# A decoder trunk on one core: the Newton steps of the final norm go from GpSimd to VectorE, and their mean squares get four buffers

## The chip, the cores and the metric

The kernel runs on one core of one Trainium2 chip. The metric is the device time of one execution in microseconds, the median of several runs; lower is better. Engines are called TensorE (PE in the profile), VectorE (DVE), ScalarE (ACT), GpSimd (POOL) and SyncE (SP). PEld is TensorE's weight load.

## The reference

One decoder layer over 2048 tokens of 1024 features: a token mixer with three head groups, then a hierarchical mixture of 32 SwiGLU experts, two for each token, then a final RMSNorm. Only the last two matter here:

```python
def rms_norm(x, g):
    xf = x.astype(jnp.float32)
    y = xf * lax.rsqrt(jnp.mean(xf * xf, axis=-1, keepdims=True) + RMS_EPS)
    return (y * g.astype(jnp.float32)).astype(x.dtype)
...
    hid = jax.nn.silu(xb @ w_gate[e]) * (xb @ w_up[e])
    return hid @ w_down[e]
...
    x = x + gt2 * hier_moe(h, router_grp_w[l], router_grp_b[l], router_exp_w[l],
                           router_exp_b[l], exp_w_gate[l], exp_w_up[l], exp_w_down[l])
return rms_norm(x, final_norm_g)
```

## The kernel before

The stages before the experts (projections, the three mixers, output projection, routing) end at about 1950 us of 3079 and are not touched. The rest is the expert stage.

**Experts.** The 32 experts are ordered by how many tokens they have, and large and small ones alternate; each has a fixed capacity, from 240 down to 66 x 2 rows for the large ones and 88 to 128 for most of the small ones. Tokens sit on the partitions, so an expert with over 128 rows has its tokens in two pieces (18 experts), one with up to 128 in one piece (14 experts). For each expert its rows of the normalised input are gathered (`gather`, line 1866), transposed on TensorE (`transpose`), multiplied by the gate and up weights (`gate_up` with line 1957 and 1959 for large experts, `gate_up_few` with line 1931 for small ones), and by the down weights (`down`, lines 162 to 164).

**Weights.** Every expert loads 12 pieces of 512 KB on SyncE's queue into a ring of 11 staging buffers, `wraw` (lines 1903 and 1918). For large experts, and for every expert's down weights, ScalarE writes a rounded high part `wh` (line 1907) and VectorE the remainder `wl` (line 1908), into rings of 8; after the remainder the staging buffer is free for the next load. Small experts use their raw gate and up pieces, eight of the eleven buffers, straight from the staging ring.

**Draining.** The gate and up products of a large expert leave PSUM by a ScalarE copy and a VectorE add into `ga_` (lines 1963 and 1964); the PSUM tiles `pg` are rings of two, which both kinds of expert share.

**The running sum and the final norm.** `yp_d` is a table in DRAM with the residual of every token. For an expert, `partial` gathers the rows of it (line 1992, on GpSimd's queue), `down` puts the expert's weighted product in `y`, and `add` (lines 1997 to 2011) adds the two (VectorE, line 2001), scatters the sum back (GpSimd, line 2004), squares it on ScalarE with the row sum in `sx` (line 2009), and turns `sx` into a mean plus epsilon (line 2010). The inverse square root comes from `rsqrt_`: a seed by integer arithmetic on VectorE (lines 61 and 62) and three Newton rounds of four instructions (lines 64 to 67) on 128 x 2 numbers. `finish`, called one expert later, multiplies by the root and the gain (VectorE, line 2017) and scatters to the output (GpSimd, line 2018), for the tokens for which this was the second expert.

**Order.** Each engine runs its instructions in a fixed order, which a list scheduler chooses when the kernel is built; semaphores hold each instruction until what it needs is there. Tiles are buffers in rings: the scheduler places the first write of a tile where it expects its buffer to come free, so a memset that needs nothing else, such as that of `sx` (line 2007), lands right behind the last reader of the ring's buffer. Transfers into one DRAM table are ordered too: a scatter into `yp_d` waits until the one before it has landed.

Of the kernel before, what the change touches and what calls it, by code (L numbers as in the profile page):

```python
# [9 lines left out]
F32 = mybir.dt.float32  # L10
# [10 lines left out]
P = 128  # L21
# [19 lines left out]
def body(tc, x, c, ada_w, ada_b, norm1_g, w_in, gla_gate_w, gla_gate_b, gla_norm_g, dsa_norm_g,  # L41
# [6 lines left out]
    V, S, G, TE = nc.vector, nc.scalar, nc.gpsimd, nc.tensor  # L48
# [5 lines left out]
    def rsqrt_(pool, ms, n, tag, rows=P, eng=None):  # L54

        E = eng or V
        sh = pool.tile([P, n], I32, name="rs_i", tag=tag + "_i")
        y_ = pool.tile([P, n], F32, name="rs_y", tag=tag + "_y")
        t_ = pool.tile([P, n], F32, name="rs_t", tag=tag + "_t")
        sh, y, t, ms = sh[:rows], y_[:rows], t_[:rows], ms[:rows]  # L60
        V.tensor_scalar(sh, ms.bitcast(I32), 1, None, op0=OP.logical_shift_right)
        V.tensor_scalar(y.bitcast(I32), sh, -1, 0x5F3759DF, op0=OP.mult, op1=OP.add)
        for _ in range(3):
            E.tensor_mul(t, y, y)
            E.tensor_mul(t, t, ms)
            E.tensor_scalar(t, t, -0.5, 1.5, op0=OP.mult, op1=OP.add)
            E.tensor_mul(y, y, t)
        return y_
# [1752 lines left out]
    mx_ = es.enter_context(tc.tile_pool(name="mx", bufs=2))  # L1821
# [175 lines left out]
    def add(st, ys, parts, after=None):  # L1997

        n, nb, pl, ix, xgs = st
        for j, (y, part) in enumerate(zip(ys, parts)):  # L2000
            a = V.tensor_add(y[:n], y[:n], part[:n])  # L2001
            if after is not None:
                tc.add_manual_dep(a.ins, after.ins.name, ORDER, reason="products first")
            G.indirect_dma_start(out=yp_d[:, :], out_offset=bass.IndirectOffsetOnAxis(ap=ix[:n, 1, j:j + 1], axis=0),  # L2004
                                 in_=y[:n], in_offset=None, bounds_check=T - 1, oob_is_err=False)
        sx = mx_.tile([P, 2], F32, name="sx")
        V.memset(sx, 1.0)
        for j, (y, part) in enumerate(zip(ys, parts)):
            S.activation(part[:n], y[:n], AF.Square, accum_out=sx[:n, j:j + 1])
        V.tensor_scalar(sx, sx, 1.0 / D, EPS, op0=OP.mult, op1=OP.add)  # L2010
        return rsqrt_(mx_, sx, 2, "rsf", eng=G)

    def finish(st, ys, parts, rs):

# [44 lines left out]
    for r in range(NE + 1):  # L2059
# [33 lines left out]
        if r:  # L2093
            fin = sts[r - 1], ys, parts, add(sts[r - 1], ys, parts, after)
# [4 lines left out]
    with tc.For_i(0, na, 1) as it:  # L2099
        itm = mo3.tile([1, 4], I32, name="itm")  # L2100
        nc.sync.dma_start(itm, it_d[bass.ds(it, 1), :])
        _, (fv,) = nc.values_load_multi_w_load_instructions(itm[0:1, 0:1], min_val=0, max_val=1)
        with tc.If(fv > 0):
            kyi = mo3.tile([P, 1], I32, name="kyi")
            nc.sync.dma_start(kyi, it_d[bass.ds(it, 1), 3:4].to_broadcast([P, 1]))
            ky = mo3.tile([P, 1], F32, name="ky")
            V.tensor_copy(ky, kyi)
            row0 = nc.sync.value_load(itm[0:1, 1:2], min_val=0, max_val=NE * T - P)
            e = nc.sync.value_load(itm[0:1, 2:3], min_val=0, max_val=NE - 1)
            pl = mo3.tile([P, 1, 2, TW], F32, name="plo")  # L2110
            G.memset(pl, 0.0)
            load_list(pl[:, 0], row0, P)
            ix = lists(mo3, pl, 1, ky[:, :, None].to_broadcast([P, 1, 2]))
            st = gather(P, pl[:, 0], ix[:, :, 0])
            xT, todo = transpose(P, st, 1)
            for f_ in todo:
                f_()
            hid, rest = gate_up_few(P, xT, weights_raw(e))
            rest()
            parts = partial(st)  # L2120
            ys = down(st, hid, weights(e, 4))
            finish(st, ys, parts, add(st, ys, parts))
# [30 lines left out]
```

## Time and profile before

| | before |
|---|---|
| median of 3 runs | 3073.16 us (3071.29 to 3079.28) |
| the profiled execution: its own time | 3080.75 us |
| its span, first to last instruction | 3079.0 us |
| busy over the span: TensorE, VectorE, ScalarE, GpSimd | 2415.8, 2043.2, 1344.5, 1095.6 us |
| mean granted TensorE clock | 0.868 of full |
| bytes moved by DMA | 479.42 MB |

The profile is one execution. Its page gives the busy time of each engine, the waits (which engine stood still, for how long, and which instruction's end let it go on: "<- POOL rs_t L65" means that the wait ended with GpSimd's instruction of line 65), and the largest groups of instructions by source line. A line can be a helper's: lines 61 to 67 are `rsqrt_` wherever it is called from. Times in a timeline count from the start of the span.

### The profile page before, as it was taken

The numbers are of one execution on the slowest core, as the hardware profiler recorded it, in microseconds if no ns is written. First come the engines' busy times: TensorE is split into PE (matmuls) and PEld (weight loads), VectorE is DVE, ScalarE is ACT, GpSimd is POOL, SyncE is SP. The second block draws the span as 40 slices with busy tenths as digits, with TensorE's granted clock in tenths as the row PEclk, the third lists the DMA queues.
The fourth block names the chain that finished last, engine by engine and source line by source line (L and its number), as shares of the span: only waits on it lengthen the run. The fifth ranks groups of instructions, "written<-read, shape, count | busy, mean of one in ns | idle before, by whom it ended". The sixth has DMA issues, their size and how long they took to land. (4 is left out here: it accounts for less than half of the span.)

```text
span 3079.0 us, 38623 instructions
## 1 busy us (share of the span) xinstructions
PE 2415.8 (78%) x12571; PEld 1885.7 (61%) x12571; DVE 2043.2 (66%) x4392; ACT 1344.5 (44%) x2339; POOL 1095.6 (36%) x1139
## 2 busy tenths in 40 slices
PE   4989868778387999578988995887887878777783
PEld 3767546777266777366766784565565656554562
DVE  6578867989889645377875666565655656554673
ACT  2577867572122243466652221443433434333451
POOL 2211224346553422465443452133232333333333
PEclk9999868889587799689998996988898989888896
DMA  7222354343411432443215434877787877776861
GB/s 208 92 82 78 114 202 141 111 142 106 139 52 59 138 120 94 125 126 111 79 59 186 156 125 129 268 231 236 238 270 226 239 225 234 214 213 195 239 191 35
DMA packets 372280, 479.42 MB, mean 156 GB/s; under 512 B 84828, under 2 KB 271356, under 8 KB 371814
## 3 DMA queue, kind: packets, MB, share of 16 engines
q1 hardware_dynamic: 334501, 421.83, 43.3%
q0 software_dynamic: 37568, 55.05, 6.7%
q8 instruction: 100, 1.64, 0.2%
q14 instruction: 111, 0.90, 0.1%
HBM read 385.75 MB, written 112.23 MB: 162 GB/s over the span
## 5 line engine op out<-in xcount | busy, mean ns | idle before, releaser
L1908 DVE TENSOR_TENSOR wl<-wraw,wh 128x1024 fp32r<-128x1024 f32 x272 | 329.4, 1221 | 209.6 <-ACT wh L1907 202.7
L1907 ACT ACTIVATE wh<-wraw 128x1024 fp32r<-128x1024 f32 x272 | 286.2, 1054 | 335.6 <-PE pd L164 119.3
L1957 PE MATMUL pg<-xT,wh 128*128 128x416 f32 (+10 forms) x1152 | 342.6, 375 | 50.0 <-DVE ga__25564 L1964 13.9
L1931 PE MATMUL pg<-wraw,xT 128*120 128x512 f32 (+9 forms) x448 | 229.1, 675 | 131.1 <-DVE ga__25236 L1964 16.2
L1959 PE MATMUL pg<-xT,wl 128*128 128x208 f32 (+10 forms) x1152 | 290.1, 252 | 0.0
L1957 PEld LDWEIGHTS pg<-xT,wh 128*128 128x128 f32 x1152 | 232.9, 202 | 58.8 <-DVE ga__25564 L1964 14.3
L441 POOL TENSOR_TENSOR xx<-xr,xx 128x1024 fp32r<-128x1024 f32 x64 | 162.1, 2534 | 269.5 <-ACT xx L440 239.8
L1931 PEld LDWEIGHTS pg<-wraw,xT 128*120 128x120 f32 (+9 forms) x448 | 88.6, 202 | 263.0 <-issue 117.9
L1959 PEld LDWEIGHTS pg<-xT,wl 128*128 128x128 f32 x1152 | 236.4, 205 | 0.6
L2004 POOL DMA_INDIRECT yp_d<-y,ix x50 | 81.8, 1637 | 398.9 <-DVE y L2001 278.1
L255 DVE SCALAR_TENSOR_TENSOR sb<-rl,iws,sb 128x1024 f32<-128x1024 f32 (+7 forms) x154 | 186.6, 1212 | 33.3 <-ACT rl L254 25.0
L162 PE MATMUL pd<-wh,hid 128*104 128x512 f32 (+17 forms) x400 | 165.5, 414 | 40.0 <-DVE y L1983 26.8
L254 ACT ACTIVATE rl<-pi,iwa 128x1024 f32<-128x1024 f32 (+7 forms) x176 | 156.9, 909 | 30.8 <-DVE sb L255 25.3
L162 PE MATMUL pp<-xx,w 128*128 128x256 f32 x512 | 155.4, 304 | 18.3 <-ACT ft L487 10.2
L163 PE MATMUL pd<-wl,hid 128*104 128x512 f32 (+17 forms) x400 | 161.7, 404 | 0.0
L164 PE MATMUL pd<-wh,hid 128*104 128x512 f32 (+17 forms) x400 | 160.9, 408 | 0.0
L163 PE MATMUL pp<-xx,w 128*128 128x256 f32 x512 | 152.8, 299 | 2.6 <-POOL xx L441 2.6
L164 PE MATMUL pp<-xx,w 128*128 128x256 f32 x512 | 152.2, 299 | 0.8 <-POOL w L468 0.8
L251 PE MATMUL pi<-iks,iqs 128*128 128x512 f32 (+3 forms) x304 | 112.2, 453 | 31.3 <-ACT rl L254 30.4
L162 PE MATMUL pj<-w,xx 128*128 128x512 f32 (+1 forms) x256 | 99.9, 392 | 40.8 <-DVE ot L208 19.4
L2018 POOL DMA_INDIRECT out_dram<-part,ix x50 | 82.6, 1653 | 123.0 <-DMA out_dram<-part,ix 45.5
L1538 DVE CUSTOM_DVE_ANT_0 pr<-ps,mk 128x512 f32<-128x512 f32 (+3 forms) x160 | 94.3, 605 | 48.2 <-PE ps L1537 27.6
(1076 smaller groups left out, 6958.9 us busy)
## 6 DMA issues: line engine op xcount, KB each, us to landing
wraw<-in_exp_w_gate_dram SPq DMA_DIRECT2D x128, 512.0 KB
wraw<-in_exp_w_up_dram SPq DMA_DIRECT2D x128, 512.0 KB
wraw<-in_exp_w_down_dram SPq DMA_DIRECT2D x128, 512.0 KB
xr<-hT_d SPq DMA_DIRECT2D x64, 512.0 KB
w<-in_ada_w_dram SPq DMA_DIRECT2D x64, 256.0 KB
w<-in_ada_w_dram SPq DMA_DIRECT2D x16, 512.0 KB
xi<-in_x_dram SPq DMA_DIRECT2D x16, 512.0 KB
hT_d<-ht SPq DMA_DIRECT2D x16, 512.0 KB
```

The lines of the kernel that those rows point to most:

```text
L162: TE.matmul(ps, st[0], mv[0], start=(k == first), stop=False, **kw)
L163: TE.matmul(ps, st[0], mv[1], start=False, stop=False, **kw)
L164: TE.matmul(ps, st[1], mv[0], start=False, stop=(k == last), **kw)
L251: TE.matmul(pi[:, s0:s0 + sl], iqs[:, h, i * P:(i + 1) * P], iks[:, g0 + s0:g0 + s0 + sl], start=True, stop=True)
L254: S.activation(rl[:, :gl], pi[:, :gl], AF.Relu, scale=iwa[:, b, h:h + 1])
L255: V.scalar_tensor_tensor(sb[:, gs], rl[:, :gl], iws[:, b, h:h + 1], (eps if h == 0 else sb)[:, gs], op0=OP.mult, op1=OP.add)
L441: G.tensor_sub(xx[1][-1], xr, xx[0][-1].bitcast(F32))
L1907: S.activation(wh, w, AF.Copy)
L1908: V.tensor_sub(wl, w, wh.bitcast(F32))
L1931: TE.matmul(pgs[a][:C], xT[:, kk], wp[2 * i + a][:, k], start=(kk == 0), stop=(kk == KD - 1))
L1957: TE.matmul(pgs[m], wh[:, k, ws], xT[:, i * 4 + k], start=(i + k == 0), stop=False, skip_group_check=True)
L1959: TE.matmul(pgs[m][:, 0], wl[:, k, ws], xT[:, i * 4 + k, 0], start=False, stop=(i + k == 4), skip_group_check=True)
```

## The change

Two edits in `add`. The mean squares `sx` get a ring of four buffers instead of the pool's two, and `rsqrt_` is called without an engine, so its three Newton rounds are emitted on VectorE, as its seed is, and no longer on GpSimd.

```diff
@@ -2003,12 +2003,12 @@
-        sx = mx_.tile([P, 2], F32, name="sx")
+        sx = mx_.tile([P, 2], F32, name="sx", bufs=4)
         V.memset(sx, 1.0)
         for j, (y, part) in enumerate(zip(ys, parts)):
             S.activation(part[:n], y[:n], AF.Square, accum_out=sx[:n, j:j + 1])
         V.tensor_scalar(sx, sx, 1.0 / D, EPS, op0=OP.mult, op1=OP.add)
-        return rsqrt_(mx_, sx, 2, "rsf", eng=G)
+        return rsqrt_(mx_, sx, 2, "rsf")
```

VectorE's order behind an expert of two pieces, before: the seed, a weight split, the first of two drains (`ga_`), the memset of a later `sx`, both products of `finish`, the second drain.

```order
4184 L61 TENSOR_SCALAR rs_i<-sx 128x2
4185 L62 TENSOR_SCALAR rs_y<-rs_i 128x2
4186 L1908 TENSOR_TENSOR wl<-wraw,wh 128x1024
4187 L1964 TENSOR_TENSOR ga__20754<-ga__20754,pg_20720 128x192
4188 L2007 MEMSET sx 128x2
4189 L2017 SCALAR_TENSOR_TENSOR part<-y,rs_y,fgr 104x1024 x2
4190 L1964 TENSOR_TENSOR ga__20754<-ga__20754,pg_20721 128x192
4191 L1908 TENSOR_TENSOR wl<-wraw,wh 128x1024 x2
```

The same place after the change, from the end of the first Newton round on:

```order
4258 L67 TENSOR_TENSOR rs_y<-rs_y,rs_t 128x2
4259 L1908 TENSOR_TENSOR wl<-wraw,wh 128x1024
4260 L64 TENSOR_TENSOR rs_t<-rs_y 128x2
4261 L65 TENSOR_TENSOR rs_t<-rs_t,sx 128x2
4262 L66 TENSOR_SCALAR rs_t<-rs_t 128x2
4263 L1964 TENSOR_TENSOR ga__20754<-ga__20754,pg_20720 128x192
4264 L67 TENSOR_TENSOR rs_y<-rs_y,rs_t 128x2
...
4268 L2007 MEMSET sx 128x2
4269 L67 TENSOR_TENSOR rs_y<-rs_y,rs_t 128x2
4270 L2017 SCALAR_TENSOR_TENSOR part<-y,rs_y,fgr 104x1024 x2
4271 L1964 TENSOR_TENSOR ga__20754<-ga__20754,pg_20721 128x192
```

The split and the first drain now stand among the twelve steps instead of ahead of the memset, and the memset still follows the last step that reads `sx`, with one step behind it. Behind experts of one piece the twelve steps stand in a row.

GpSimd's order at an expert of two pieces, before: two gathers for a coming expert, two scatters into the running sum, then the steps (the first of twelve shown).

```order
589 L1866 DMA xg<-h_d,ix_19725 96x1024 x2
590 L2004 DMA yp_d<-y,ix_18730 2049x1024 x2
591 L64 TENSOR_TENSOR rs_t<-rs_y 128x2
...
602 L67 TENSOR_TENSOR rs_y<-rs_y,rs_t 128x2
603 L1992 DMA part<-yp_d,ix_18730 100x1024
604 L2018 DMA out_dram<-part,ix_18730 2048x1024 x2
```

After:

```order
541 L1866 DMA xg<-h_d,ix_19725 96x1024 x2
542 L2004 DMA yp_d<-y,ix_18730 2049x1024 x2
543 L1992 DMA part<-yp_d,ix_18730 100x1024
544 L2018 DMA out_dram<-part,ix_18730 2048x1024 x2
545 L1866 DMA xg<-h_d,ix_19725 104x1024
```

The steps are gone and the order of GpSimd's transfers is the same. SyncE's order is unchanged; TensorE's and ScalarE's differ at one place near the end, where the last experts' transposes stand a few rows earlier.

## Rows read from the trace of the kernel before

**Rows 1.** Busy time of the expert stage: PE, PEld, DVE, ACT, POOL, clock, DMA share, GB/s.
```profile
1958.00:3024.00 1066.00, 854.02 (x4202) 623.39 (x4200) 622.08 (x930) 424.80 (x680) 341.80 (x542) 0.88 0.74 225
```
**Rows 2.** VectorE's waits, 1950 to 3079 us: total us, times, longest us.
```profile
DVE wl L1908 <- ACT wh L1907: 181.7, 94, 9.9
DVE sx L2007 <- POOL rs_t L65: 155.0, 29, 12.1
...
DVE part L2017 <- POOL rs_y L67: 23.3, 30, 5.2
```
**Rows 3.** VectorE's timeline at one place: start, duration, instruction, [idle before <-releaser].
```profile
2192.94 0.17 DVE L62 TENSOR_SCALAR rs_y<-rs_i 128x2 int32<-128x2 int32 x1
...
2194.19 0.35 DVE L1964 TENSOR_TENSOR ga__20754<-ga__20754,pg 128x192 f32<-128x192 f32 x1
2202.78 0.06 DVE L2007 MEMSET sx<- 128x2 f32 x1 [8.25 <-POOL rs_t L65]
2203.30 2.48 DVE L2017 SCALAR_TENSOR_TENSOR part<-y,rs_y,fgr 104x1024 f32<-104x1024 f32 x2 [0.46 <-POOL rs_y L67]
2205.70 0.35 DVE L1964 TENSOR_TENSOR ga__20754<-ga__20754,pg 128x192 f32<-128x192 f32 x1
2205.97 1.22 DVE L1908 TENSOR_TENSOR wl<-wraw,wh 128x1024 fp32r<-128x1024 f32 x1
```
**Rows 4.** GpSimd's timeline at the same place.
```profile
2189.60 3.93 POOL L2004 DMA_INDIRECT yp_d<-y,ix  x1 [0.31 <-issue]
2198.98 1.02 POOL L2004 DMA_INDIRECT yp_d<-y,ix  x1 [5.45 <-issue]
2200.01 0.22 POOL L64 TENSOR_TENSOR rs_t<-rs_y 128x2 f32<-128x2 f32 x1
...
2203.08 0.19 POOL L67 TENSOR_TENSOR rs_y<-rs_y,rs_t 128x2 f32<-128x2 f32 x1
```
**Rows 5.** Busy time of four microseconds of that stall, columns as in rows 1.
```profile
2202.00:2206.00 4.00, 1.50 (x12) 1.26 (x10) 2.75 (x5) 0.00 (x0) 2.79 (x7) 0.91 0.00 1
```
**Rows 6.** SyncE's timeline behind that stall.
```profile
2214.22 4.66 SPq L1903 DMA_DIRECT2D wraw<-in_exp_w_gate_dram  x2
```
**Rows 7.** TensorE's timeline: the first matmuls of three small experts.
```profile
2157.14 15.83 PE L1931 MATMUL pg<-wraw,xT 128*104 128x512 f32 x32 [8.68 <-DVE ga__20416 L1964]
...
2223.66 16.69 PE L1931 MATMUL pg<-wraw,xT 128*104 128x512 f32 x32 [6.52 <-DVE ga__20968 L1964]
...
2287.63 2.89 PE L1931 MATMUL pg<-wraw,xT 128*108 128x512 f32 x3 [7.95 <-DVE ga__21503 L1964]
```
**Rows 8.** VectorE's timeline at the places before and after: two two-piece memsets, one one-piece place.
```profile
2133.77 0.06 DVE L2007 MEMSET sx<- 128x2 f32 x1 [9.20 <-POOL rs_t L65]
...
2237.34 0.06 DVE L2007 MEMSET sx<- 128x2 f32 x1 [2.81 <-POOL rs_t L65]
...
2240.47 0.69 DVE L1934 TENSOR_TENSOR sg<-sg,pg 104x512 f32<-104x512 f32 x1 [1.31 <-PE pg L1931]
...
2265.62 0.06 DVE L2007 MEMSET sx<- 128x2 f32 x1 [3.73 <-POOL rs_t L65]
```
**Rows 9.** VectorE's timeline at the last two places.
```profile
3035.75 2.48 DVE L2017 SCALAR_TENSOR_TENSOR part<-y,rs_y,fgr 68x1024 f32<-68x1024 f32 x2 [5.06 <-POOL rs_y L67]
...
3061.18 2.48 DVE L2017 SCALAR_TENSOR_TENSOR part<-y,rs_y,fgr 66x1024 f32<-66x1024 f32 x2 [5.23 <-POOL rs_y L67]
```
**Rows 10.** VectorE's timeline, first stage: a root computed on VectorE, nine rows, first and last.
```profile
24.36 0.17 DVE L318 TENSOR_SCALAR ss<-ss 128x2 f32<-128x2 f32 x1 [1.02 <-ACT jk L317]
...
25.96 0.16 DVE L65 TENSOR_TENSOR rs_t<-rs_t,ss 128x2 f32<-128x2 f32 x1
```
**Rows 11.** VectorE's timeline, sparse attention stage: a step of another root.
```profile
1324.70 1.11 DVE L64 TENSOR_TENSOR rs_t<-rs_y 128x2 f32<-128x2 f32 x1
```
**Rows 12.** GpSimd's timeline beside it.
```profile
1323.19 2.61 POOL L128 TENSOR_TENSOR acc<-acc,w 128x512 f32<-128x512 f32 x2
```
**Rows 13.** Line 2001 in the expert stage: ns shortest/median/longest, first and last start, forms.
```profile
L2001 DVE TENSOR_TENSOR y<-y,part x50: 1209/1216/1232, 1979.0 to 3052.9; 104x1024 f32<-104x1024 f32 x8, 88x1024 f32<-88x1024 f32 x7, 120x1024 f32<-120x1024 f32 x5, 96x1024 f32<-96x1024 f32 x4
```

## The prediction

> **What bounds the kernel now.** I read the expert stage alone, since nothing before it changes. Over its 1066 us TensorE is busy for 854.0 and VectorE for 622.1 (58%); the DMA engines are busy for 0.74 of it [rows 1]. No engine is full, so the question is what each waits for.
>
> In VectorE's waits [rows 2] two lines belong to this change. The memset of the mean squares waits 29 times for GpSimd's Newton steps, 155.0 us in all, up to 12.1 us at once; the product that uses the finished root waits 30 more times, 23.3 us. Together that is 178.3 us in which VectorE, whose order is fixed, does nothing.
>
> One such place shows how [rows 3]. VectorE has the seed of the root at 2192.94, splits one weight tile, drains one PSUM tile at 2194.19, and then stands still for 8.25 us in front of a memset of 0.06 us, and for another 0.46 us in front of the product. Behind these two in its queue stand the second drain (2205.70) and the next weight split (2205.97).
>
> GpSimd shows why it takes so long [rows 4]. Its twelve steps take only some 3 us, but they stand behind two scatters into the running sum, and the second scatter starts at 2198.98, after a first that took 3.93 us to issue and some five us of waiting that the trace gives no engine for. In the built program that second scatter waits for the first one's transfer to land. So arithmetic that needs only the seed is queued behind a DMA landing.
>
> Does the stall reach the end? Follow what is queued behind it. The split at 2205.97 frees a staging buffer, which lets the next weights be requested; in the last four microseconds of the stall the DMA engines moved nothing (share 0.00 [rows 5]). Three down loads, their splits, then the next gate loads at 2214.22 [rows 6], then the splits of these with a drain of PSUM between them, and only then can TensorE start the next small expert, at 2223.66 after 6.52 us of idling [rows 7].
>
> That chain has a fixed length. From the end of the memset's wait to the small expert's first matmul it is 20.9 us after a stall of 8.25 (2202.78 to 2223.66) and 22.0 us after one of 3.73 (2265.62 to 2287.63) [rows 3, 7, 8]. From that matmul to the next stall's beginning it is 37.4 us (2157.14 to 2194.53) and 38.2 us (2223.66 to 2261.89). A pair of experts thus costs about 59 us plus the stall. The pair that ends with 8.25 us of stall took 69.0 us (2133.77 to 2202.78), the one that ends with 3.73 took 62.8. So I count a microsecond of this stall as a microsecond of the kernel.
>
> **The change, part by part.**
>
> *What goes.* There are 32 places, 18 behind experts of two token pieces and 14 behind experts of one. A one-piece place waits 2.81 us for the memset and some 0.46 for the product, the same each time (the memset at 2237.34 in [rows 8]). 13 of the 29 memset waits are of that kind, 13 x 2.81 = 36.5 us; the other 16 are two-piece places with 155.0 - 36.5 = 118.5 us. The last two places have no memset to wait on; their products wait 5.06 and 5.23 us [rows 9], 10.3 together. Of the remaining 13.0 us of product waits, shared by 28 places, the two-piece places have some 15 x 0.46 = 7. Two-piece places: 118.5 + 10.3 + 7 = 135.8 us.
>
> *What comes.* 12 steps per place on VectorE, each needing the one before. Where VectorE ran such a chain earlier in this kernel, the starts run from 24.36 to 25.96 [rows 10], nine rows with eight spacings of 0.20 us; I take 0.20. A place costs 12 x 0.20 = 2.4 us, 18 places 43.2 us. The order puts a weight split and a drain among the steps, which hides a tenth of a microsecond or two; I leave that out.
>
> *One-piece places.* 3.27 us go and 2.4 come, 0.9 us x 14 = 12 us at most. But the next thing there, the product of gate and up, waits for the small expert's matmuls (1.31 us of idling at 2240.47 [rows 8]), so the saving only lengthens that wait. I take 0 and keep 12 us as a bound.
>
> *Four buffers.* I take 0. The order of the changed kernel has the memset in the same place, after the last step that reads the buffer, and now all these are on VectorE, so it waits for nothing with two buffers or four. Nor would four have helped alone: the product, two rows behind the memset, needs the root itself, which comes half a microsecond later [rows 3].
>
> *GpSimd's queue.* It loses 384 steps and gains nothing, so its gathers of the running sum come up to 3 us earlier unless the scatter's landing holds them. I take 0. SyncE's order does not change.
>
> **Sum:** -135.8 + 43.2 = -92.6 us, rounded to -92. The profiled execution took 3080.75 us with a span of 3079.0, so it would take 2989. It lies 7.6 us over the median of the runs, 3073.16, and 1.5 over the slowest of them (3079.28); I put the forecast on the median: **2981 us**. Its own bounds: if all 178.3 us went and the steps cost only their 0.16 us busy time, 384 x 0.16 = 61.4, the gain is 117 (2956); if 0.4 us per step, 86.4, the gain is 49 (3024). I stay near 0.20 because the spacing row is this same helper on the same two columns.
>
> *A rule against it.* VectorE has 622 of 1066 us busy, against GpSimd's 341.8, and the work goes from the idler engine to the busier [rows 1]. The Trainium skill ("Perfetto Trace Analysis", Optimizing Scalar/DVE Operations) says that offloading to GpSimd may make sense where VectorE is saturated, though the two share a read port. VectorE at 58%, with 178 us of its idle time in these very waits, is not saturated, so I side with the rows; what the rule would make of the time is a rival below. The same section gives some 60 ns of data access per small VectorE instruction on SBUF; as an estimate from that page the steps would be 18 x 12 x 0.06 = 13 us and the gain 123, but no row has dependent steps that close.
>
> **The rivals.**
>
> *Half given back.* While VectorE stands, the scatter and the gathers have the DMA engines to themselves; without the stall they run beside the weight loads, and the 21 us chain to the next expert stretches. For: the first scatter's issue took 3.93 us amid other work, the second 1.02 in the quiet [rows 4]. Against: the chain is no longer after a stall of 3.73 us than after 8.25. If half of the gain is lost: 3073 - 46 = 3027.
>
> *More than the sum.* The one-piece places count too and the steps cost only their busy time: 2956, from above.
>
> *The stall is cover.* Weight loads set the pace, and what VectorE wins here it loses in its largest wait, that for ScalarE's weight halves, 181.7 us [rows 2]: 3073, no change. Against: a DMA share of 0.00 inside the stall [rows 5].
>
> *VectorE is the bound, slower.* As before, but the new steps also delay splits and drains that are late already: +43, 3116. It decides where splits queue behind busy work on VectorE instead of waiting for ScalarE. Against: 58% busy. This is what the rule of the Trainium skill ("Perfetto Trace Analysis", Optimizing Scalar/DVE Operations) on a saturated VectorE amounts to.
>
> *Steps stretched on VectorE, slower.* In an earlier stage the same helper on the same two columns had a step of 1.11 us on VectorE at 1324.70 [rows 11], while GpSimd ran adds on 512 columns [rows 12]. If GpSimd's issuing of indirect transfers does the same here, at 1.1 us a step a two-piece place costs 13.2 us and the 18 places 237.6, against 135.8 removed: +102, 3175 us. It decides from 135.8 / (18 x 12) = 0.63 us a step. Against it: the add of the running sum, on two inputs from SBUF and often beside a scatter being issued, took 1209 to 1232 ns in all 50 cases [rows 13], and the seed at 2192.94, on one input, ran its 0.17 us inside the scatter's issue of 2189.60 to 2193.53 [rows 3, 4]. The Trainium skill ("SBUF — State Buffer", Who interferes with whom) says that a VectorE instruction contends with GpSimd if it has two SBUF inputs, then only with GpSimd instructions that read SBUF, or if it runs in a mode that takes both ports, as tensor-scalar forms may. The stretched step beside GpSimd's adds agrees with that; the unstretched seed shows that issuing alone did not do it there.
>
> **How the numbers follow.** Forecast (2955 to 3005) 0.60; half given back 0.18; more than the sum 0.11; cover 0.04; VectorE the bound 0.03; stretched 0.04. A difference under 0.3% (9 us) is no difference here. Faster: 0.60 + 0.18 + 0.11 = 0.89; same 0.04; slower 0.07. The range takes the forecast's own bounds, most of the half case and part of the larger gain: 2950 to 3032, which leaves out the last three cases and the tails, just under 0.2.
>
> **What would show it.** In the changed profile the memset and the product no longer wait for GpSimd; VectorE's Newton steps in this stage start 0.20 us apart; the time from the seed to the first product is about 4 us at two-piece places, with a split and a drain inside it, instead of 6 to 14; pairs of experts take 60 to 63 us; the stage is some 90 us shorter, with the same wait for gate loads in front of small experts. Wrong would be: steps near 1 us (stretched), the 21 us chain grown to 25 or more (given back), or the same pair length with longer waits for weights (cover).

## The result and the profile after

| | before | after |
|---|---|---|
| median | 3072.22 us (4 runs, 3068.59 to 3079.28) | 2963.58 us (4 runs, 2958.76 to 2966.22) |
| the profiled execution: its own time, its span | 3080.75, 3079.0 us | 2962.22, 2960.3 us |
| first small expert's first matmul to the last product (line 2017) | 1949.42 to 3061.18: 1111.8 us | 1943.38 to 2943.21: 999.8 us |

The ratio is 0.9642, 95% interval 0.962 to 0.9664: 108.6 us between the medians. The two profiled executions differ by more, 118.5 us; 6.0 of it lie ahead of the expert stage (the last row, which begins there, differs by 112.0).

The changed expert stage, the window of [rows 1] less 6 us at the start and with its end as far ahead of the last product; columns as there.

```profile
1952.00:2906.00 954.00, 829.54 (x4155) 600.19 (x4154) 673.17 (x1283) 425.99 (x676) 260.66 (x182) 0.93 0.83 251
```

112 us shorter, VectorE at 71% instead of 58%, the DMA engines' share 0.83 instead of 0.74. VectorE's waits, 1940 to 2961 us (total us, times, longest us), against [rows 2]:

```profile
DVE wl L1908 <- ACT wh L1907: 170.8, 92, 12.9
DVE y L2001 <- DMA part<-yp_d,ix: 32.3, 14, 8.4
DVE y L1983 <- PE pd L164: 25.9, 15, 4.6
```

The two waits for GpSimd are gone, 178.3 us of them, and no new large one took their place. The place that answers to [rows 3], in VectorE's timeline (start, duration, instruction, idle before):

```profile
2169.84 0.17 DVE L62 TENSOR_SCALAR rs_y<-rs_i 128x2 int32<-128x2 int32 x1
2170.04 0.16 DVE L64 TENSOR_TENSOR rs_t<-rs_y 128x2 f32<-128x2 f32 x1
...
2170.74 1.23 DVE L1908 TENSOR_TENSOR wl<-wraw,wh 128x1024 fp32r<-128x1024 f32 x1
...
2172.35 0.35 DVE L1964 TENSOR_TENSOR ga__20754<-ga__20754,pg 128x192 f32<-128x192 f32 x1
...
2173.30 0.06 DVE L2007 MEMSET sx<- 128x2 f32 x1
2173.40 0.16 DVE L67 TENSOR_TENSOR rs_y<-rs_y,rs_t 128x2 f32<-128x2 f32 x1
2173.59 2.48 DVE L2017 SCALAR_TENSOR_TENSOR part<-y,rs_y,fgr 104x1024 f32<-104x1024 f32 x2
2175.99 0.35 DVE L1964 TENSOR_TENSOR ga__20754<-ga__20754,pg 128x192 f32<-128x192 f32 x1
2176.26 1.22 DVE L1908 TENSOR_TENSOR wl<-wraw,wh 128x1024 fp32r<-128x1024 f32 x1
```

Seed to product took 10.36 us and takes 3.75, with the split and the drain among the steps. GpSimd there, against [rows 4]:

```profile
2166.81 3.63 POOL L2004 DMA_INDIRECT yp_d<-y,ix  x1 [3.61 <-DMA part<-yp_d,ix]
2175.84 1.14 POOL L2004 DMA_INDIRECT yp_d<-y,ix  x1 [5.40 <-DVE part L2017]
2180.67 1.00 POOL L1992 DMA_INDIRECT part<-yp_d,ix  x1 [3.69 <-DMA yp_d<-y,ix]
2181.97 1.00 POOL L2018 DMA_INDIRECT out_dram<-part,ix  x1 [0.30 <-DVE ga__20754 L1967]
2190.00 1.00 POOL L2018 DMA_INDIRECT out_dram<-part,ix  x1 [7.02 <-DVE wl L1908]
```

The second scatter still starts 9.0 us after the first (9.4 before), but nothing of VectorE's stands behind it any more. That it waits for a landing is shown by the trace of the kernel with four buffers alone (below), which records the landings: at its first 14 two-piece places the second scatter starts 0.8 to 0.9 us after the first has landed. The gate load in SyncE's timeline and the small expert's matmuls in TensorE's, against [rows 6, 7]:

```profile
2185.00 4.10 SPq L1903 DMA_DIRECT2D wraw<-in_exp_w_gate_dram  x2
```

```profile
2193.18 16.71 PE L1931 MATMUL pg<-wraw,xT 128*104 128x512 f32 x32 [7.70 <-DVE ga__20968 L1964]
```

From the seed to that matmul it was 30.7 us and is 23.3. A one-piece place, against [rows 8], and the last place, against [rows 9], in VectorE's timeline:

```profile
2206.56 0.17 DVE L62 TENSOR_SCALAR rs_y<-rs_i 128x2 int32<-128x2 int32 x1
...
2209.14 1.29 DVE L2017 SCALAR_TENSOR_TENSOR part<-y,rs_y,fgr 104x1024 f32<-104x1024 f32 x1
...
2940.62 0.17 DVE L62 TENSOR_SCALAR rs_y<-rs_i 128x2 int32<-128x2 int32 x1
...
2943.21 2.48 DVE L2017 SCALAR_TENSOR_TENSOR part<-y,rs_y,fgr 66x1024 f32<-66x1024 f32 x2
```

Where nothing stands between, twelve steps take 2.4 us from the end of the seed, 0.20 apart, as forecast.

### The profile page after: what moved, and what is told of

The parts are those of the page before. It is cut to its first block, busy times and chain, and to the rows that moved or that the text cites. A ratio compares the mean times of both kernels' runs of the same rounds, so it can differ in the third digit from the quotient of the medians.

```text
span 2960.3 us, 38558 instructions
## 1 busy us (share of the span) xinstructions
PE 2385.6 (81%) x12571; PEld 1857.5 (63%) x12571; DVE 2103.6 (71%) x4776; ACT 1346.8 (45%) x2339; POOL 1010.4 (34%) x755
## 5 line engine op out<-in xcount | busy, mean ns | idle before, releaser
L1957 PE MATMUL pg<-xT,wh 128*128 128x416 f32 (+10 forms) x1152 | 324.3, 361 | 18.6 <-DVE xT L1889 11.5
L1931 PE MATMUL pg<-wraw,xT 128*120 128x512 f32 (+9 forms) x448 | 231.0, 679 | 88.1 <-DVE ga__18823 L1964 11.1
L1959 PE MATMUL pg<-xT,wl 128*128 128x208 f32 (+10 forms) x1152 | 283.2, 246 | 0.0
L1957 PEld LDWEIGHTS pg<-xT,wh 128*128 128x128 f32 x1152 | 223.2, 194 | 24.8 <-DVE xT L1889 14.0
L1959 PEld LDWEIGHTS pg<-xT,wl 128*128 128x128 f32 x1152 | 226.6, 197 | 0.4
L2004 POOL DMA_INDIRECT yp_d<-y,ix x50 | 97.6, 1952 | 309.6 <-DVE y L2001 170.3
L254 ACT ACTIVATE rl<-pi,iwa 128x1024 f32<-128x1024 f32 (+7 forms) x176 | 157.0, 910 | 30.7 <-DVE sb L255 27.7
L1992 POOL DMA_INDIRECT part<-yp_d,ix x50 | 65.9, 1319 | 178.6 <-DMA yp_d<-y,ix 169.4
```

The costliest lines, as they stand in the source:

```text
L254: S.activation(rl[:, :gl], pi[:, :gl], AF.Relu, scale=iwa[:, b, h:h + 1])
L1931: TE.matmul(pgs[a][:C], xT[:, kk], wp[2 * i + a][:, k], start=(kk == 0), stop=(kk == KD - 1))
L1957: TE.matmul(pgs[m], wh[:, k, ws], xT[:, i * 4 + k], start=(i + k == 0), stop=False, skip_group_check=True)
L1959: TE.matmul(pgs[m][:, 0], wl[:, k, ws], xT[:, i * 4 + k, 0], start=False, stop=(i + k == 4), skip_group_check=True)
```

## The experiments

The forecast's gain was 92 us and the measured one 109. The runs ask which step was wrong by those 16 us. Each was timed beside the kernel before. An edit is shown against the changed kernel unless the text says otherwise, and `...` marks lines left out. The first four ran on one chip (its kernel before: 3075.36 us), the next four on another (3081.15), the last four together (3077.09).

### Four buffers alone

```diff
-        return rsqrt_(mx_, sx, 2, "rsf")
+        return rsqrt_(mx_, sx, 2, "rsf", eng=G)
```

> The kernel before with four buffers for the mean squares and nothing else; the Newton steps stay on GpSimd. My theory (the product needs the root itself, so the wait only moves from the memset to the product two rows behind it): no change, 3072 +- 9 us, and in VectorE's waits the 155 us of the memset now stand at the product. Rival (the ring of two was what held VectorE, the buffers carry a share of the gain): the two-piece places lose most of 118 us, 2960 to 3020 us.

Measured: 3078.18 us, ratio 1.0004 (0.9984 to 1.0024). The buffers alone do nothing. VectorE's waits, 1950 to 3073 us:

```profile
DVE sx L2007 <- POOL rs_t L65: 151.6, 28, 12.6
DVE part L2017 <- POOL rs_y L67: 30.2, 31, 5.3
```

But the wait did not move to the product, as I expected. In the built order the memset of a later expert now stands there, still right behind the last step that reads the current one's buffer.

### The steps alone

```diff
-        sx = mx_.tile([P, 2], F32, name="sx", bufs=4)
+        sx = mx_.tile([P, 2], F32, name="sx")
```

> The changed kernel with the ring of mean squares back at two buffers; only the move to VectorE is left. My theory: the memset stands behind the last step that reads its buffer, on the same engine, so it waits for nothing: 2964 +- 9 us. Rival (four buffers carry the 16 us that the gain of 109 had beyond the forecast's 92): about 2980 us.

Measured: 2965.25 us, 0.9626 (0.9599 to 0.9654). The move to VectorE is the whole gain.

### One-piece places back on GpSimd

```diff
-        return rsqrt_(mx_, sx, 2, "rsf")
+        return rsqrt_(mx_, sx, 2, "rsf", eng=None if len(ys) == 2 else G)
```

> The changed kernel with the steps of the 14 one-piece places put back on GpSimd. The forecast's term (one-piece places cost nothing either way, the next row there waits for TensorE's products): 2964 +- 5 us. Rival A (they count in full, which would be 12 of the missing 16 us): 14 x 0.9 = 12 us more, 2976 us, with 2.8 us of memset wait at each of these places.

Measured: 2963.48 us, 0.9621 (0.9594 to 0.9648), no different from the steps alone on the same chip. The seed-to-product times of the 14 places rose from 37.5 us in all to 52.4, and the kernel did not notice: the forecast's zero holds, and rival A falls.

### Steps on GpSimd, ahead of the second scatter

```diff
-            G.indirect_dma_start(out=yp_d[:, :], out_offset=bass.IndirectOffsetOnAxis(ap=ix[:n, 1, j:j + 1], axis=0),
-                                 in_=y[:n], in_offset=None, bounds_check=T - 1, oob_is_err=False)
+            sc = lambda j=j, y=y: G.indirect_dma_start(out=yp_d[:, :], out_offset=bass.IndirectOffsetOnAxis(ap=ix[:n, 1, j:j + 1], axis=0),
+                                                       in_=y[:n], in_offset=None, bounds_check=T - 1, oob_is_err=False); j or sc()
...
-        return rsqrt_(mx_, sx, 2, "rsf")
+        rs = rsqrt_(mx_, sx, 2, "rsf", eng=G); len(ys) == 2 and tc.add_manual_dep(sc().ins, last[0].ins.name, ORDER, reason="steps first"); return rs
```

`last[0]` is the last Newton step (the lines that set it are left out).

> The steps stay on GpSimd, with four buffers, but the second scatter into the running sum is placed behind the twelve steps instead of ahead of them. My theory (the steps were not slow, they were queued behind the landing of the first scatter): a two-piece place then waits some 3.3 us, as a one-piece place does, so against the changed kernel 18 x (3.3 - 2.4) = 16 us more if all of it counts: 2964 to 2980 us. Rival 1 (GpSimd's steps themselves are the cost): near 3072 us. Rival 2 (the second scatter, now later, holds up the next gather of the running sum and with it VectorE's add): waits of the add for the gather grow from 32 us by 2 to 3 us at each place, 3000 to 3030 us.

Measured: 3002.62 us, 0.9753 (0.9729 to 0.9778). GpSimd's and then VectorE's timeline at the same place:

```profile
2173.08 3.93 POOL L2004 DMA_INDIRECT yp_d<-y,ix  x1 [0.30 <-issue]
2177.03 0.78 POOL L64 TENSOR_TENSOR rs_t<-rs_y 128x2 f32<-128x2 f32 x1
...
2180.66 0.20 POOL L67 TENSOR_TENSOR rs_y<-rs_y,rs_t 128x2 f32<-128x2 f32 x1
2181.76 1.35 POOL L2004 DMA_INDIRECT yp_d<-y,ix  x1 [0.91 <-DMA yp_d<-y,ix]
```

```profile
2180.89 1.28 DVE L2017 SCALAR_TENSOR_TENSOR part<-y,rs_y,fgr 104x1024 f32<-104x1024 f32 x1 [3.14 <-POOL rs_y L67]
```

The stall falls from 8.7 us to 3.14 without a step leaving GpSimd, and the kernel gains 73 us. So two thirds of the gain are to be had by order alone: the steps were queued behind a landing, which is now named in the row of the second scatter. VectorE's order is not the same, though. The first drain, which the changed kernel has ahead of the product (2172.35 above), stands behind it here, as at 10 of the first 13 two-piece places:

```profile
2182.09 0.35 DVE L1964 TENSOR_TENSOR ga__20754<-ga__20754,pg 128x192 f32<-128x192 f32 x1
```

This kernel is 37 us behind the changed one, in the range of my rival 2 and not for its reason: VectorE's add waits less for its gather (15.0 us), not more. What grew is the way from the product to the small expert, and VectorE's wait for ScalarE at line 1969 (53.0 us against 24.1). How much of the 37 us the later drains cost, no run separates.

### Steps doubled at two-piece places

```diff
-        for _ in range(3):
+        for _ in range(rounds):
...
-        return rsqrt_(mx_, sx, 2, "rsf")
+        return rsqrt_(mx_, sx, 2, "rsf", rounds=6 if len(ys) == 2 else 3)
```

> The changed kernel with six Newton rounds instead of three at the 18 two-piece places: 12 more dependent steps on VectorE there, values the same to rounding. The forecast's price (0.20 us a step, all on the path): 18 x 12 x 0.20 = 43 us more, 3007 us. Rival B (the steps lie largely beside waits for weights that VectorE would have anyway, which would be the missing 16 us): a third to a half of it, 2978 to 2987 us.

Measured: 2996.16 us, 0.9723 (0.9699 to 0.9747). The changed kernel was not timed on this chip. Against its medians on the two others this is 31 to 33 us more, by the ratios 25 to 30, and against the next kernel below, which ran beside this one, 39. The forecast's price made 43 and rival B 14 to 23. For 216 more steps it is 0.12 to 0.18 us each.

But not only the steps differ. At 12 of the first 13 two-piece places a further weight split, and at most of them the second drain too, now stands among the steps instead of behind the product. VectorE's timeline at the place that answers to [rows 3], with the product last:

```profile
2173.11 1.23 DVE L1908 TENSOR_TENSOR wl<-wraw,wh 128x1024 fp32r<-128x1024 f32 x1
...
2174.33 0.34 DVE L1964 TENSOR_TENSOR ga__20802<-ga__20802,pg 128x192 f32<-128x192 f32 x1
...
2175.46 2.48 DVE L2017 SCALAR_TENSOR_TENSOR part<-y,rs_y,fgr 104x1024 f32<-104x1024 f32 x2
```

### Steps doubled at one-piece places

The same, with `len(ys) == 1`.

> The changed kernel with six Newton rounds instead of three at the 14 one-piece places. The forecast's term (what is saved or spent there only changes the wait for the small expert's products): 2964 +- 5 us. Rival A (these places count in full): 14 x 12 x 0.20 = 34 us more, 2997 us.

Measured: 2957.03 us, 0.9601 (0.9579 to 0.9623). Seed to product rose from 37.5 to 72.8 us over these places, at no cost. That is the forecast's zero a second time, from the other side.

### Three instructions a round, and two rounds

```diff
             E.tensor_mul(t, y, y)
-            E.tensor_mul(t, t, ms)
-            E.tensor_scalar(t, t, -0.5, 1.5, op0=OP.mult, op1=OP.add)
-            E.tensor_mul(y, y, t)
+            E.tensor_mul(t, t, ms) if tag != "rsf" else E.scalar_tensor_tensor(t, t, -0.5, ms, op0=OP.mult, op1=OP.mult)
+            E.tensor_scalar(t, t, -0.5, 1.5, op0=OP.mult, op1=OP.add) if tag != "rsf" else E.scalar_tensor_tensor(y, t, 1.5, y, op0=OP.add, op1=OP.mult)
+            tag != "rsf" and E.tensor_mul(y, y, t)
```

The tag "rsf" is this root's. The second kernel has also the seed constant 0x5F1FFFF9, and two rounds with (-0.703952253, 1.68191391) and (-0.5, 1.5).

> The changed kernel with three instructions a round instead of four (the factor -0.5 and the addition of 1.5 ride on the two products), 9 dependent steps a place instead of 12, values the same to rounding. The forecast's price: 18 x 3 x 0.20 = 11 us less, 2953 us. With the one-piece places counting too: 32 x 3 x 0.20 = 19 us less, 2944 us. Rival B (steps covered): 2958 to 2964 us.

> As the fused one, with two rounds instead of three from a better seed constant (relative error of the root below 1e-6 by arithmetic): 6 dependent steps a place instead of 12. The forecast's price: 18 x 6 x 0.20 = 22 us less, 2942 us. With the one-piece places: 32 x 6 x 0.20 = 38 us less, 2925 us. Rival B (steps covered): 2953 to 2964 us.

Measured: 2949.86 us, 0.957 (0.9544 to 0.9596), and 2949.54 us, 0.957 (0.9548 to 0.9593). Both lie 14 to 16 us below the changed kernel's 2963.58 and 2965.45 and are the fastest of the study, but those ran on other chips. By the ratios it is 17 to 22 us, and against the kernel with doubled one-piece steps, which ran beside them, 7. The second gains nothing more for its three steps less, though the first one's runs reach from 2940 to 2960 us, so its share is not sharp. For the second kernel's 108 steps less that is 0.07 to 0.21 us each. Here too the scheduler moved more than the steps: at the first three two-piece places of the first kernel, and the first five of the second, the first drain stands behind the product, and a few rows of the last experts stand otherwise. ScalarE's waits for gate loads over the expert stage show what stands in the steps' place; first the changed kernel, then the one with two rounds:

```profile
ACT wh L1907 <- DMA wraw<-in_exp_w_gate_dram: 55.6, 28, 5.5
```

```profile
ACT wh L1907 <- DMA wraw<-in_exp_w_gate_dram: 73.6, 27, 10.6
```

VectorE is sooner through, and 18 us more go to waiting for these loads. Over all weight loads, however, ScalarE waits 157.7 us in the first profile and 156.8 in the second (and 170.5 with the two-piece steps doubled), so it is not shown that an earlier VectorE only waits longer for weights.

### Without output scatters

```diff
-            G.indirect_dma_start(out=oflat, out_offset=bass.IndirectOffsetOnAxis(ap=ix[:n, 2, j:j + 1], axis=0),
+            len(ys) == 2 or G.indirect_dma_start(out=oflat, out_offset=bass.IndirectOffsetOnAxis(ap=ix[:n, 2, j:j + 1], axis=0),
```

in the changed kernel, in the one with the steps ahead of the second scatter, and in the kernel before; and the changed kernel itself again. The three leave out the output scatters behind two-piece experts and nothing else, and each keeps the order of the kernel that it comes from.

> The changed kernel without the 36 scatters of finished rows to the output behind two-piece experts (those rows of the output are not written). Over 13 pairs, from the seed of the root to the next small expert's first matmul, the changed kernel takes 23.1 us a pair. Contention theory (GpSimd's transfers beside the weight loads lengthen this stretch; here the first output scatter starts some 8 us and the second some 16 us behind the product, the second mostly behind the gate loads): little is won, up to 1 us a pair, 2945 to 2964 us. Rival (these transfers never mattered): 2964 us, 23.1 us a pair.

> The kernel with the steps on GpSimd ahead of the second scatter, without the 36 output scatters behind two-piece experts. With them it took 3003 us, 38 more than the changed kernel's order, of which 18 x (3.3 - 2.1) = 21 us at most are the steps themselves; a pair took 26.4 us from seed to small expert, 10.4 us of it from the first gate load's request. Contention theory (five of GpSimd's transfers fall into that stretch): both output scatters out of it win 1.5 to 2.5 us a pair, 2965 to 2980 us, and the gate stretch falls to 8 to 9 us. Rival (the 38 us are VectorE's idling alone): 3003 us less what the changed kernel wins without them, the difference of the two stays at 38.

> The kernel before without the 36 output scatters behind two-piece experts. There both scatters fall between the product and the request of the next gate loads (12.7 us a pair, against 11.0 in the changed kernel). Contention theory (that is the 1.7 us a pair, 22 us in all, which the forecast did not have): this stretch falls to about 11 us and the kernel to 3040 to 3055 us. Rival (the stretch is longer for another reason, the splits' own order): no change beyond what the changed kernel wins, 3065 to 3075 us.

> The changed kernel itself, on the same chip as the three others, as their measure: 2964 +- 9 us; it also tells whether the doubled steps (2996), the fused ones (2950) and the two rounds (2950), which ran on another chip, stand 32 us above and 14 below it.

Measured: changed 2952.13 us (0.9578, 0.9549 to 0.9607), steps first 2992.06 (0.9713, 0.9683 to 0.9743), before 3050.59 (0.9891, 0.9861 to 0.9921), changed again 2965.45 (0.9626, 0.9596 to 0.9655).

In the three without these scatters some 10 us go at the very end, where the last output scatters close the kernel (from the last product to the end of the span 17.8 us before, and 6.6 without them). What is left is read from the profiles. The table splits 13 pairs of experts by three starts: the seed at a two-piece place (line 62), its first product (line 2017), the small expert's first matmul (line 1931). A pair runs from one two-piece place's first product to the next one's, so that the first column is that of the place which ends it. Means of one pair in us, from one profile of each kernel; the last column is the stage, from the first small expert's first matmul to the last row of products:

| kernel | seed to product | product to small expert | small expert to next seed | 13 pairs | stage |
|---|---|---|---|---|---|
| before | 9.80 | 20.80 | 38.96 | 904.4 | 1111.8 |
| buffers alone | 10.05 | 20.58 | 39.18 | 907.6 | 1110.2 |
| changed | 4.02 | 19.08 | 39.25 | 810.6 | 999.8 |
| changed again | 4.02 | 19.33 | 39.18 | 813.1 | 998.6 |
| two-piece steps doubled | 8.22 | 16.09 | 39.46 | 829.2 | 1027.7 |
| two rounds | 2.42 | 21.19 | 38.62 | 808.9 | 985.5 |
| steps first | 4.40 | 21.90 | 38.03 | 836.3 | 1034.3 |
| before, no output scatters | 10.26 | 21.14 | 37.53 | 896.1 | 1094.7 |
| changed, no output scatters | 4.06 | 20.86 | 37.92 | 817.0 | 999.7 |
| steps first, no output scatters | 4.41 | 22.82 | 37.34 | 839.4 | 1031.3 |

In the stage the output scatters cost the kernel before 16 us (1110 to 1112, then 1094.7) and the changed kernel nothing. By the medians of the whole kernels leaving them out gains 26.5 us before and 13.3 after the change, a difference of 13; by the ratios it is 19, give or take 16, just clear of the noise. So without these scatters the change is worth 98.5 us (3050.59 to 2952.13), and 95.0 in the stage. Their place in the queues, GpSimd's timeline of before behind the product of 2203.30 [rows 3]:

```profile
2205.82 1.01 POOL L2018 DMA_INDIRECT out_dram<-part,ix  x1 [0.30 <-DVE part L2017]
2211.53 0.99 POOL L2018 DMA_INDIRECT out_dram<-part,ix  x1 [4.70 <-DVE y L1983]
```

They stood 2.5 and 8.2 us behind the product, and now stand 8.4 and 16.4 behind it, the second behind the gate loads' request. My contention theory had the size right and the place wrong: without them the stretch from the product to the small expert got no shorter in any kernel; the time is won from the small expert to the next seed. In the changed kernel that stretch falls as much (39.25 to 37.92), but the way to the small expert takes it back (19.08 to 20.86). Why stays open. And the steps-first kernel keeps its distance (1031.3 against 999.7, and 39.9 us between the medians), so these scatters are not what holds it back: that rival stands. Of its 37 us the way from seed to product has 6.4 over the 18 places (77.7 against 71.3); the rest stands behind the product, and its cause is open.

## Why the prediction was right, and where it was off

**What bounds.** "I count a microsecond of this stall as a microsecond of the kernel": borne out, and a little more than that. Seed to product lost 5.8 us a pair, and the pair lost 7.2. "That chain has a fixed length" was read from two places. Over the 13 pairs of the kernel before, the way from the product to the small expert runs from 17.3 to 26.2 us, 20.8 on average, with no tie to the length of the stall ahead of it; after the change it is 19.1 on average.

**What goes and what comes, locally.** Seed to product over the 18 two-piece places was 162.3 us and is 71.3: 91.0 less, against the sum of 92.6. The spacing of 0.20 us holds.

**Where the missing 16 us lie.** The 13 pairs gave 94 us. Of these 75 came from seed to product and 22 from the product to the small expert (20.80 to 19.08), and 4 were lost behind it. The sum had nothing for that second stretch. Two of its terms may be behind the difference, and no run decides between them.

*The price of a step on the path* may be too high. I put 12 x 0.20 us a place on the path in full. By the doubled steps a step costs 0.12 to 0.18 us, and the 43.2 us of the sum would be 25 to 39: 4 to 18 of the missing 16. By the two rounds it costs 0.07 to 0.21. But in all these kernels splits and drains have changed places with the product: with the steps doubled, 4.2 us more between seed and product and 3.1 less behind it are in part a split and a drain that now stand in the first stretch. So the price is not measured by itself.

*GpSimd's queue, "I take 0"*, may be wrong. What the term names came out: the gather of the running sum (line 1992) starts 10.8 us behind the seed, as it did before (10.9), now held by the scatter's landing. But it took no account of the output scatters behind it, which now start later. Without them the change is worth 95.0 to 98.5 us, close to the sum of 92.6, and the way from the product to the small expert is nearly the same before and after (21.14 and 20.86). So some 13 to 16 us of the gain are there only with these scatters. By what mechanism is not shown. The rival "half given back" had this term with the other sign.

Each of the two could cover most or all of the 16 us, and both in full would overshoot them. So the forecast was right in its mechanism, the stall that goes and the steps that come, and the cause of the remaining 16 us stays open. One sign did not come as written: "the same wait for gate loads in front of small experts". TensorE idled 131.1 us ahead of the small experts' matmuls before and 88.1 after.

**One-piece places 0, four buffers 0**: both shown, the first from both sides. The reason given for the buffers (the product needs the root) was not tested, because the memset stayed where it was.

**The rivals.** "Cover", "VectorE the bound" and "steps stretched" are excluded by the time, and the last also by the 384 steps themselves, which took 0.16 us at the median and 0.39 at most; "half given back" by the time. "More than the sum" (2956) is nearer to the measured 2964 than the forecast (2981). Of its two reasons the first falls, for the one-piece places do not count; the second, steps that cost only their 0.16 us, is not excluded by 0.12 to 0.18. The rule that speaks against the move, of the Trainium skill ("Perfetto Trace Analysis", Optimizing Scalar/DVE Operations), is about a saturated VectorE; at 71% of the stage after the move it still waits 170.8 us for ScalarE alone.

## What to carry to other kernels

Small arithmetic on an engine whose queue also issues dependent transfers inherits their landing times; look at what stands ahead of it in that queue, not at its busy time. Even on the same engine, two thirds of the gain here came from putting it ahead of the waiting transfer. And where a scheduler orders the program, doubling or halving a piece of work prices it only if the rest of the order stays: here splits and drains moved each time, so compare the orders before the times.

## What was not expected of the hardware

TensorE ran the stage's 4268 matmuls in 858.4 us of busy time instead of 877.5, though nothing on it changed: the granted clock, a mean over its levels of 1.2 and 2.4 GHz, was 0.92 over the stage and 0.88 before. The place of [rows 3] shows where it fell. From the seed to the product TensorE is busy throughout, at a granted clock of 1.00; then it stands still for 2.60 us for the second drain, which is queued behind the product, and from 2206.11 to 2213.00 the clock is 0.57 and matmuls of the same shape take longer. After the change it does not stand still there. TensorE's timeline, before and after:

```profile
2203.05 0.36 PE L1957 MATMUL pg<-xT,wh 128*128 128x384 f32 x1
...
2206.11 0.69 PE L1957 MATMUL pg<-xT,wh 128*128 128x384 f32 x1 [2.60 <-DVE ga__20754 L1964]
...
2206.75 0.57 PE L1957 MATMUL pg<-xT,wh 128*128 128x384 f32 x1
```

```profile
2176.43 0.36 PE L1957 MATMUL pg<-xT,wh 128*128 128x384 f32 x1
```

Over the 13 stretches from the product to the small expert the mean granted clock was 0.77 before and 0.92 after, and 0.86 in the steps-first kernel, whose stretch is the longest of the three. At the place shown the slower matmuls delay nothing that VectorE shows: from the product to line 1967 it is 7.76 us both times. So part of the return may be clock, but over the stage no run separates it.
